# State-space mixer: the pair's rotation, additions and scan in place in PSUM on VectorE, the products for the transposed matrix on GpSimd

## The chip, the cores and the metric

One core of one Trainium2 chip runs one launch of the kernel. The metric is the device time of the launch in microseconds (us).

## The reference

One inference step of a model of two layers. Layer 0 mixes tokens by a state-space mixer (S5), layer 1 by a Fourier mixer; each mixer is followed by a gated feed-forward network with a convolution. There are 1152 tokens (128 of a context, 1024 of a sample) of 1024 channels. Only the S5 mixer is touched:

```python
def s5_direction(u, lam_re, lam_im, log_dt, b_re, b_im, c_re, c_im, h0, reverse):
    ...
    abar = jnp.exp(lam * dt)
    bbar = ((abar - 1.0) / lam)[..., None] * bmat
    bu = jnp.einsum('blgc,gpc->blgp', u.astype(jnp.complex64), bbar)
    ...
    _, h = lax.associative_scan(_linear_recurrence, (a, bu), axis=1, reverse=reverse)
    y = jnp.real(jnp.einsum('gcp,blgp->blgc', cmat, h))
```

So in each of 64 groups of 16 channels, a complex state h of 64 elements runs along the sequence as h = abar h + bu, once forwards and once backwards; y is the sum over both directions, and the last states are outputs too. After it come a gelu, the matmul `z = y @ w_glu` (GLU), and the rest of the network.

## The kernel before

**Tiling.** Tokens are taken in chunks of 8. The input of a group is then a tile u of 128 partitions (8 tokens x 16 channels) by 146 columns (`KW`: 144 chunks and two more for the ends). The eight groups of a block are worked off as four *pairs* of groups; 8 blocks of 4 pairs are 32 pairs, numbered i = 4b + pr. The two groups of a pair lie in the two halves of the 128 partitions (64 states each); each tile has both directions (dr) and the real and the imaginary part (r).

**What a block needs first** (`tables`, `make_ca`, `make_p`, `make_t`, `make_u`). The tables cs and sn (cosine and sine of the phase per chunk: VectorE computes and wraps the phase, L1306, L1307, L980, L981; ScalarE takes the absolute value wa, L1312, and the sines, L1320); Bbar (tiles Bb and Bx, L1381 to L1383 and what follows); CA (the output matrix times powers of abar, on GpSimd, L1365 to L1369); the products P of Bbar with powers of abar (VectorE, L1409 and six of 512 elements on L1414, three for each half of the block), which TensorE transposes (L1422) and ScalarE copies to PT (L1425); T, the part of y that stays within a chunk (64 small matmuls L1444, copies kc L1454 to L1456 on ScalarE, an addition on GpSimd, stored to DRAM and read back by SP's queue); and the next u (`make_u`, copies hb on ScalarE, L1476).

**A pair.** `vmm`: sixteen matmuls make V = PT u (L1499) in a two-bank PSUM tile; two such tiles take turns. `vin`: VectorE multiplies V by the sine and by the cosine (B L1521, A L1522), GpSimd adds the products into the SBUF tile Z (L1523, L1524), ScalarE makes the decay tile dec (L1514, needs no data of the pair), copies the final states out (Fin, L1526), GpSimd clears a column (L1527), ScalarE writes the initial states (L1528). The rotation thus takes the phase out, so that what is left is a real recurrence. `vout`: VectorE scans Z into S (L1538: one instruction over 592 elements, both parts and directions one behind the other, with zeros in dec and the Z columns at the borders) and rotates back, C1 and C2 (L1543 to L1545). `wmm`: TensorE makes y from C, CA, T and u (L1561), and ScalarE copies it to ysb (L1567).

**What sets the order.** The schedule is by hand: each engine runs its instructions in the order in which the program issues them, and waits at semaphores. `Ssm.run` is the loop. Step i issues the V matmuls of pairs up to i + 2 (as soon as their PT is there), `vin(i + 1)`, `wmm(i - 1)`, then what the next blocks need by pr (pr 0: tables, first half of the products, pr 1: second half, pr 2: Bbar, pr 3: the next u), then `vout(i)`, and behind it the work called late:

```python
late = tr[0] + tb[2:3]                            # pr 0: transposes of half 0, sines
late = tr[1] + tb[3:]                             # pr 1: transposes of half 1, cosines
late = [lambda: self.make_t(b + 1)()]             # pr 2: T of the next block
```

From pair 27 on, the loop also issues first work of the next stage (`early`), and when the last `wmm` is issued, the GLU follows (L199).

Of the kernel before, what the change touches and what calls it, by code (L numbers as in the profile page):

```python
# [959 lines left out]


class Ssm:
    def __init__(self, net, k_dram, y_dram, out_re, out_im):
# [147 lines left out]
    def start(self):  # L1111

        nc, sp = self.nc, self.sp

        mask = self.mask = sp.tile([128, 2, 148], F32, name="mask")
        nc.gpsimd.memset(mask, 1.0)
        for dr, p in ((0, 0), (0, 130), (1, 0), (1, 18)):
            nc.gpsimd.memset(mask[:, dr, p:p + 1], 0.0)
        self.Z = [sp.tile([128, 2, 2, 148], F32, name=f"Z{i}") for i in range(2)]
        for z in self.Z:  # L1120
            nc.gpsimd.memset(z[:, :, :, 147], 0.0)
            nc.gpsimd.memset(z[:, :, :, 0], 0.0)
        self.Fin = sp.tile([128, 2, NG], F32, name="Fin")
        self.hb = self.sg.tile([128, 8, KW], F32, name="hb")
        nc.gpsimd.memset(self.hb[:, :, 128:130], 0.0)
# [24 lines left out]
    def powers(self, gs, beside=None):  # L1150
# [3 lines left out]
        n = gs.stop - gs.start  # L1154
        PR = sp.tile([128, n, 9], F32, tag="A", bufs=2, name="PR")
        PI = sp.tile([128, n, 9], F32, tag="B", bufs=2, name="PI")
        t = sp.tile([128, n, 8], F32, tag="C1", bufs=2, name="q1")
        V.memset(PR[:, :, 0], 1.0)
# [85 lines left out]
    def ada_mm(self, n, p):  # L1244

        two = len(p.shape) == 3
        ps, q = ([p[:, g, 292:420] for g in range(2)], p[:, 0, 420:424]) if two else ([p[:, :128], p[:, 128:256]], p[:, 256:260])
        w = self.wa.pop(n)
        for v, o in enumerate(ps):
            for k in range(8):  # L1250
                j = 32 * (k % 4)
                self.nc.tensor.matmul(o[j:j + 32], lhsT=self.n.SC[:, k], rhs=w[:, k, 128 * v:128 * v + 128], start=k < 4,
                                      stop=k >= 4)
        m = self.sg.tile([128, 256], F32, tag="m", bufs=2, name="m_ada")
        if two:
            self.nc.scalar.activation(m.rearrange("p (v f) -> p v f", v=2), p[:, :, 292:420], AF.Copy)
        else:
            self.nc.scalar.activation(m, p[:, :256], AF.Copy)
        self.m_ada.append((n, q, m))
# [135 lines left out]
    def make_p(self, b):  # L1395
# [6 lines left out]
        x = [t[:, :, None, :].to_broadcast([128, 8, 8, 16]) for t in (Bb[:, 0, :, 0], Bx[:, 1], Bx[:, 0])]  # L1402
        qs, Ps = [], {}

        def prod(h, i):
            def f():
                if not qs:
                    qs.append(self.sg.tile([128, 8, 8], F32, tag="gs", bufs=1, name="gs"))
                    V.tensor_tensor(qs[0], self.G[:, 0, gs], self.G[:, 1, gs], OP.add)  # L1409
                if i == 0:  # L1410
                    Ps[h] = self.sg.tile([128, 3, 4, 8, 16], F32, tag="P", bufs=1, name="P")
                g = (qs[0], self.G[:, 1, gs], self.G[:, 0, gs])[i]
                hs = slice(4 * h, 4 * h + 4)
                V.tensor_tensor(Ps[h][:, i], g[:, hs, :, None].to_broadcast([128, 4, 8, 16]), x[i][:, hs], OP.mult)  # L1414
            return f
# [74 lines left out]
    def vmm(self, i):  # L1490
# [4 lines left out]
        for dr in range(2):  # L1495
            for ri in range(2):
                for a in range(2):
                    r, x = slice(64 * a, 64 * a + 64), u[:, 2 * pr + a]
                    nc.tensor.matmul(V[r, dr, ri * KW:(ri + 1) * KW], lhsT=PT[pr // 2][:, ri, 2 * (pr % 2) + dr, r],  # L1499
                                     rhs=x[:, ::-1] if dr else x, start=True, stop=True)  # L1500
        self.vd[i] = V
        if 1 < i < 7:
            self.ada_mm(i + 1, V)
            if i < 5:
                self.ada_load(i + 3)

    def vin(self, i):
        nc, sp = self.nc, self.sp
        b, pr = divmod(i, 4)
        cs, sn = self.tab[b]  # L1510
        V = self.vd.pop(i)
        dec = self.sp.tile([128, 2, 2, 148], F32, tag="dec", bufs=2, name="dec")
        for dr in range(2):
            nc.scalar.activation(dec[:, :, dr], self.mask[:, None, dr].to_broadcast([128, 2, 148]), AF.Copy,  # L1514
                                 scale=self.r8[:, 2 * i + dr:2 * i + dr + 1])
        A = sp.tile([128, 2, 2, KW], F32, tag="A", bufs=2, name="A")
        B = sp.tile([128, 2, 2, KW], F32, tag="B", bufs=2, name="B")
        Z = self.Z[i % 2]
        v = V[:, :, :2 * KW].rearrange("p g (r k) -> p g r k", r=2)
        bc = lambda t: t[:, 2 * pr:2 * pr + 2, 1:147][:, :, None, :].to_broadcast([128, 2, 2, KW])  # L1520
        nc.vector.tensor_tensor(B, v, bc(sn), OP.mult)  # L1521
        nc.vector.tensor_tensor(A, v, bc(cs), OP.mult)  # L1522
        nc.gpsimd.tensor_tensor(Z[:, 0, :, 1:147], A[:, :, 0], B[:, :, 1], OP.add)  # L1523
        nc.gpsimd.tensor_tensor(Z[:, 1, :, 1:147], A[:, :, 1], B[:, :, 0], OP.subtract)  # L1524
        zf = Z.rearrange("p r d k -> p r (d k)")
        nc.scalar.activation(self.Fin[:, :, 2 * i:2 * i + 2], zf[:, :, 129:166:36], AF.Copy)  # L1526
        nc.gpsimd.memset(Z[:, :, 0, 130], 0.0)  # L1527
        nc.scalar.activation(zf[:, :, 0:167:166], self.h0[:, :, 2 * i:2 * i + 2], AF.Copy)  # L1528
        self.zd[i] = (Z, dec)

    def vout(self, i):
        nc, sp = self.nc, self.sp
        b, pr = divmod(i, 4)
        cs, sn = self.tab[b]
        Z, dec = self.zd.pop(i)
        S = sp.tile([128, 2, 2, 148], F32, tag="S", bufs=2, name="S")
        f = lambda t: t.rearrange("p r d k -> p (r d k)")
        nc.vector.tensor_tensor_scan(f(S), f(dec), f(Z), 0.0, OP.mult, OP.add)  # L1538
        C1 = sp.tile([128, 2, 2, KW], F32, tag="C1", bufs=2, name="C1")
# [41 lines left out]
    def run(self):  # L1581
        self.TB = 2
        for nm in ("tab", "BC", "xb", "CA", "Bb", "Bx", "PT", "T", "U", "vd", "zd", "cd", "ysb"):
            setattr(self, nm, {})
# [51 lines left out]
        n = 32  # L1636
        nv, ready = 2, {0}
        for i in range(n + 1):
            b, pr = divmod(i, 4)
            n1, n2 = b + 1 < 8, b + 2 < 8  # L1640
            while nv < n and nv <= i + 2 and nv // 4 in ready:
                self.vmm(nv)
                nv += 1
            if i + 1 < n:
                self.vin(i + 1)
            if i:
                self.wmm(i - 1)
# [31 lines left out]
            if pr == 1:  # L1679
                if n1:  # L1680
                    call(pp[1])
                    late = tr[1] + tb[3:]
                    if not n2:
                        late.append(lambda: self.make_t(b + 1)())
                    ready.add(b + 1)
                if not b:
# [5 lines left out]
            if pr == 2:  # L1692
                if n1 and n2:
                    late = [lambda: self.make_t(b + 1)()]
                if n2:
# [6 lines left out]
            if pr == 3 and n2:  # L1702
                self.make_u(b + 2)
                pl = ca[4:] + [ends]
                if b + 3 < 8:
                    self.load_x(b + 3)
            call(pl[:1])
            self.vout(i)
            call(pl[1:])
            if i == n - 1:  # L1710
# [156 lines left out]
```

## Time and profile before

| | before |
|---|---|
| median of 3 runs | 2461.51 us (2460.70 to 2462.96) |
| the profiled execution | 2462.09 us |
| its span | 2460.3 us |
| its mean granted TensorE clock | 0.978 |
| TensorE matmuls, busy | 2315.1 us (94%) |
| VectorE, busy | 1562.1 us (63%) |
| ScalarE, busy | 857.3 us (35%) |
| GpSimd, busy | 754.2 us (31%) |

The span runs from the first to the last instruction that the profile shows; the execution's own time is 1.8 us longer. The shares are means over the whole launch: the mixer's 32 pairs lie between about 48 and 347 us, where VectorE is busiest, and behind them TensorE works nearly without a gap. A time in the trace counts from the start of the span. In the rows, PE is TensorE, DVE is VectorE, ACT ScalarE, POOL GpSimd; a tile's row reads output <- inputs, with partitions x elements.

### The profile page before, as it was taken

To read this page: it belongs to the slowest core of one execution; us is meant where nothing else is said; L and a number is where in the kernel's file an instruction comes from. 1 tells how busy PE (TensorE), PEld (TensorE's weight loads), DVE (VectorE), ACT (ScalarE), POOL (GpSimd) and SP (SyncE) were. 2 spreads that over 40 slices of the span, in tenths; PEclk is the share of its full clock that TensorE was granted. 3 is DMA by queue.
4 is the path that set the end of the run, shared out by engine and by line. 5 is a ranking of instruction groups with operands and counts; after the bars stand their busy time and mean duration, and the time that the engine had idled before them with its cause. 6 is when DMAs were issued, how large, how long until landed. Compare 5 with 4: busy or idle time off the path is not lost.

```text
span 2460.3 us, 35710 instructions
## 1 busy us (share of the span) xinstructions
PE 2315.1 (94%) x14754; PEld 2229.3 (91%) x14754; DVE 1562.1 (63%) x2385; ACT 857.3 (35%) x1251; POOL 754.2 (31%) x517
## 2 busy tenths in 40 slices
PE   4787899999999999999999999999999999999996
PEld 3676789778999999999999989899999999999996
DVE  8999977888555553555535574954554545545456
ACT  4444463234422233222322354442233222332234
POOL 6667631345211221112211253621122111221124
PEclk8888899999999999999999999999999999999998
DMA  6323278573101111011110121111111101111012
GB/s 213 122 59 81 75 206 296 198 246 110 51 27 43 43 52 44 26 43 43 52 44 27 61 97 36 52 46 34 42 52 45 42 27 43 52 43 41 29 44 77
DMA packets 94522, 182.33 MB, mean 74 GB/s; under 512 B 16948, under 2 KB 57204, under 8 KB 93336
## 3 DMA queue, kind: packets, MB, share of 16 engines
q1 hardware_dynamic: 90824, 170.67, 22.0%
q0 software_dynamic: 2096, 6.62, 0.8%
q8 instruction: 117, 1.92, 0.3%
q10 hardware_dynamic: 1440, 2.75, 0.3%
q14 instruction: 45, 0.37, 0.0%
HBM read 163.70 MB, written 11.53 MB: 71 GB/s over the span
## 4 chain that ended last, share of the span: by engine, by line
PE 69%; DVE 22%; issue 4%; ACT 1%; DMA 1%; POOL 1%; SPq 1%; DVEq 0%; ACTq 0%; POOLq 0%
PE acc L199 64%; DVE c L308 3%; DVE S L1538 2%; DVE P L1414 2%; PE f L839 2%; DVE dh L602 1%; DVE dl L602 1%; DVE X L916 1%; DVE C L1545 1%; DVE C L1543 1%; DVE h L222 1%; PE f L749 1%; DVE X L363 1%; DVE X L364 1%; DVE B L1521 1%
## 5 line engine op out<-in xcount | busy, mean ns | idle before, releaser
L199 PE MATMUL acc<-h,uh 128*128 128x384 f32 (+1 forms) x4992 | 1014.9, 338 | 0.5 <-ACT ysb L1567 0.5
L199 PEld LDWEIGHTS acc<-h,uh 128*128 128x128 f32 x4992 | 884.9, 188 | 15.3 <-issue 12.3
L183 POOL TENSOR_TENSOR ul<-raw,uh 128x1024 fp32r<-128x1024 f32 x104 | 280.1, 2693 | 1238.8 <-ACT uh L182 1238.8
L199 PE MATMUL acc<-h,ul 128*128 128x384 f32 (+1 forms) x2496 | 571.2, 337 | 0.0
L308 DVE SCALAR_TENSOR_TENSOR c<-t,cw,c 128x896 f32<-128x896 f32 x704 | 347.2, 562 | 202.6 <-ACT c L305 202.6
L199 PEld LDWEIGHTS acc<-h,ul 128*128 128x128 f32 x2496 | 448.2, 189 | 0.0
L182 ACT ACTIVATE uh<-raw 128x1024 fp32r<-128x1024 f32 x108 | 113.7, 1053 | 544.7 <-PE acc L199 505.5
L300 DVE COPY wb<-acc 128x2 f32<-128x2 f32 x88 | 13.9, 158 | 406.0 <-PE acc L199 406.0
L363 DVE SCALAR_TENSOR_TENSOR X<-acc,MOD,X 128x768 f32<-128x768 f32 x168 | 169.7, 1010 | 118.3 <-PE acc L199 118.3
L199 PE MATMUL acc<-gh,dh 128*128 128x384 f32 x960 | 220.7, 337 | 18.4 <-DVE X L365 18.4
L199 PE MATMUL acc<-gl,dh 128*128 128x384 f32 x960 | 218.5, 335 | 0.0
L199 PE MATMUL acc<-gh,dl 128*128 128x384 f32 x960 | 218.2, 334 | 0.0
L199 PEld LDWEIGHTS acc<-gh,dh 128*128 128x128 f32 x960 | 168.8, 188 | 26.9 <-PE acc L199 23.6
L199 PEld LDWEIGHTS acc<-gh,dl 128*128 128x128 f32 x960 | 171.4, 188 | 0.0
L199 PEld LDWEIGHTS acc<-gl,dh 128*128 128x128 f32 x960 | 171.2, 188 | 0.0
L336 ACT ACTIVATE gh<-c 128x1152 fp32r<-128x1152 f32 x44 | 51.4, 1169 | 329.2 <-DVE c L331 290.9
L303 ACT ACTIVATE t<-t,wb 128x1024 f32<-128x1024 f32 x88 | 101.4, 1152 | 152.6 <-DVE t L301 152.6
L183 POOL TENSOR_TENSOR dl<-raw,dh 128x1024 fp32r<-128x1024 f32 x40 | 99.8, 2514 | 165.3 <-ACT dh L182 165.3
L305 ACT ACTIVATE c<-t,cb,cw 128x1152 f32<-128x1152 f32 x88 | 118.8, 1351 | 2.9
L301 DVE TENSOR_TENSOR t<-acc,R 128x1152 f32<-128x1152 f32 x88 | 118.6, 1348 | 0.0
L326 ACT ACTIVATE c<-c 128x1152 f32<-128x1152 f32 x44 | 51.4, 1167 | 152.9 <-DVE c L308 152.9
L1561 PE MATMUL y<-C,CA 64*128 64x146 f32 x1024 | 77.6, 305 | 14.1 <-DVE C L1543 14.1
(324 smaller groups left out, 2765.4 us busy)
## 6 DMA issues: line engine op xcount, KB each, us to landing
raw<-w_up SPq DMA_DIRECT2D x88, 512.0 KB, 3.6
w_ada<-w_ada SPq DMA_DIRECT2D x80, 512.0 KB, 4.7
raw<-w_down SPq DMA_DIRECT2D x44, 512.0 KB, 3.6
w_ada<-w_ada SPq DMA_DIRECT2D x8, 1024.0 KB, 6.4
raw<-w_glu SPq DMA_DIRECT2D x16, 512.0 KB, 4.7
u<-hb SPq DMA_DIRECT2D x64, 73.0 KB, 2.8
y_scratch<-ysb SPq DMA_DIRECT2D x8, 584.0 KB, 3.4
xt<-x SPq DMA_DIRECT2D x9, 512.0 KB, 8.4
```

What stands on the lines that cost most here:

```text
L182: nc.scalar.activation(hi, raw, AF.Copy)
L183: (E or nc.gpsimd).tensor_tensor(lo, raw, hi.bitcast(F32), OP.subtract)
L199: mm(outs[j], lhsT=w, rhs=r[j], start=first and i == 0, stop=last and i == 2)
L301: nc.vector.tensor_tensor(t.rearrange("p (a b) -> p a b", a=3), p[:, :, :384], self.R.rearrange("p (a b) -> p a b", a=3), OP.mult)
L303: nc.scalar.activation(t[:, :NS], t[:, :NS], AF.Identity, bias=wb[:, 0:1])
L305: nc.scalar.activation(c, t, AF.Identity, bias=cb[:, ui:ui + 1], scale=w(1))
L308: nc.vector.scalar_tensor_tensor(o, a, w(i), o, op0=OP.mult, op1=OP.add)
L326: nc.scalar.activation(c, c, AF.Silu)
L336: nc.scalar.activation(gh, c, AF.Copy)
L363: nc.vector.scalar_tensor_tensor(v, p[:, 0:2, :384], s(0), v, op0=OP.mult, op1=OP.add)
L602: nc.vector.scalar_tensor_tensor(o, i, a, o, op0=OP.mult, op1=OP.add)
L1561: nc.tensor.matmul(yp[:, a, :KW], lhsT=CA[64 * a:64 * a + 64, ca, 2 * pr + dr, 1:9].rearrange("p a b -> p (a b)"), rhs=x[:, ::-1] if dr el ...
```

## The change

`view` takes 592 contiguous elements of the two-bank tile V, from element V0 = 216 on: the real part of both directions ends the first bank, the imaginary part begins the second, and every direction has 148 columns, two of them gaps. All steps of a pair work in that view:

- ScalarE zeroes the gaps (one instruction of 4 x 2 elements, L1527 of the changed kernel).
- `vin`: B = V times sine goes to SBUF (L1532), V times cosine back into V (L1533), and the two additions, now on VectorE, take V and B into V (L1534, L1535). ScalarE copies Fin out (L1537), clears the column (L1538) and writes the initial states (L1539).
- `scan`, now a function of its own, scans V in place (L1543); `vout` reads the states from V (L1554 to L1556).
- Z, A and S are gone, and B has one buffer. dec has two more zeros.

The order of a step becomes: V matmuls of pair i + 1 alone (if not issued yet), `scan(i)`, `vin(i + 1)`, `vout(i)`, `wmm(i - 1)`, then the next blocks' work. The products P are issued on GpSimd for blocks 2 to 7 (L1412, L1417) and stay on VectorE for blocks 0 and 1. The transposes of the second half move from pr 1 to pr 2, right ahead of `make_t`; T of block 7 moves from pair 25 to pair 26. The small columns of the modulation matmuls (`ada_mm`), which share the tile V in the first pairs, move to the free places of its banks, with two copies for one. The tiles of the powers (`powers`) get places of their own.

```diff
 def ada_mm(self, n, p):
-        ps, q = ([p[:, g, 292:420] for g in range(2)], p[:, 0, 420:424]) if two else ...
+        ps, q = ([p[:, 0, 0:128], p[:, 1, 300:428]], p[:, 0, 128:132]) if two else ...
...
-            self.nc.scalar.activation(m.rearrange("p (v f) -> p v f", v=2), p[:, :, 292:420], AF.Copy)
+            for v in range(2):
+                self.nc.scalar.activation(m[:, 128 * v:128 * v + 128], ps[v], AF.Copy)
 def make_p(self, b):
+        E = nc.gpsimd if b > 1 else V
...
-                    V.tensor_tensor(qs[0], self.G[:, 0, gs], self.G[:, 1, gs], OP.add)
+                    E.tensor_tensor(qs[0], self.G[:, 0, gs], self.G[:, 1, gs], OP.add)
...
-                V.tensor_tensor(Ps[h][:, i], g[:, hs, :, None].to_broadcast([128, 4, 8, 16]), x[i][:, hs], OP.mult)
+                E.tensor_tensor(Ps[h][:, i], g[:, hs, :, None].to_broadcast([128, 4, 8, 16]), x[i][:, hs], OP.mult)
 def vmm(self, i):
+                    o = 148 * dr + 1 + (0 if ri else V0)
+                    nc.tensor.matmul(V[r, ri, o:o + KW], lhsT=PT[pr // 2][:, ri, 2 * (pr % 2) + dr, r],
+    def view(self, V):
+        return V.rearrange("p g k -> p (g k)")[:, V0:V0 + 592]
 def vin(self, i):
+        f = V.rearrange("p g k -> p (g k)")
+        nc.scalar.activation(f[:, V0 + 147:V0 + 147 + 592].rearrange("p (s k) -> p s k", k=148)[:, :, 0:2],
+                             self.zero[:, None, :].to_broadcast([128, 4, 2]), AF.Copy)
...
         nc.vector.tensor_tensor(B, v, bc(sn), OP.mult)
-        nc.vector.tensor_tensor(A, v, bc(cs), OP.mult)
-        nc.gpsimd.tensor_tensor(Z[:, 0, :, 1:147], A[:, :, 0], B[:, :, 1], OP.add)
-        nc.gpsimd.tensor_tensor(Z[:, 1, :, 1:147], A[:, :, 1], B[:, :, 0], OP.subtract)
+        nc.vector.tensor_tensor(v, v, bc(cs), OP.mult)
+        nc.vector.tensor_tensor(v[:, 0], v[:, 0], B[:, 1], OP.add)
+        nc.vector.tensor_tensor(v[:, 1], v[:, 1], B[:, 0], OP.subtract)
...
-        nc.gpsimd.memset(Z[:, :, 0, 130], 0.0)
+        nc.scalar.activation(zf[:, :, 130], self.zero, AF.Copy)
+    def scan(self, i):
+        S = self.view(self.vd[i])
+        self.nc.vector.tensor_tensor_scan(S, self.dec.pop(i).rearrange("p r d k -> p (r d k)"), S, 0.0, OP.mult, OP.add)
 def run(self):
-            while nv < n and nv <= i + 2 and nv // 4 in ready:
+            if nv < n and nv <= i + 1:
                 self.vmm(nv)
                 nv += 1
+            if i < n:
+                self.scan(i)
             if i + 1 < n:
                 self.vin(i + 1)
+            if i < n:
+                self.vout(i)
             if i:
                 self.wmm(i - 1)
...
             if pr == 1:
-                    late = tr[1] + tb[3:]
-                    if not n2:
-                        late.append(lambda: self.make_t(b + 1)())
-                    ready.add(b + 1)
+                    late = tb[3:]
...
             if pr == 2:
-                if n1 and n2:
-                    late = [lambda: self.make_t(b + 1)()]
+                if n1:
+                    late = tr[1] + [lambda: self.make_t(b + 1)()]
```

In the rows of order, a number behind a tile's name is its buffer, the bracket names the engines or DMA queues at whose semaphores the instruction waits, and the scan stands as SCALAR_TENSOR_TENSOR.

**Order, first place: VectorE around a block's tables.** Before, from the rotation of the block's second pair to the first product behind the scan of its first:

```order
L1521 TENSOR_TENSOR B<-V,sn 128x584 [waits PE_49]
L1522 TENSOR_TENSOR A<-V,cs 128x584
L1306 COPY w<-W_173 128x8x18
L1307 TENSOR_TENSOR w<-W_173,ph_174 128x8x112
L980 TENSOR_SCALAR wa<-w 128x8x112 [waits DVE_49]
L981 TENSOR_TENSOR w<-w,wa 128x8x112 [waits DVE_49]
L1409 TENSOR_TENSOR gs<-Gt 128x64
L1414 TENSOR_TENSOR P<-gs,Bb 128x512 [waits DVE_49]
L1414 TENSOR_TENSOR P<-Gt,Bx 128x512 x2
L1538 SCALAR_TENSOR_TENSOR S<-dec,Z_133 128x592 [waits Activation_49,Pool_49]
L1543 TENSOR_TENSOR C_2419<-S,cs 128x584 [waits DVE_49,PE_49]
```

Now, from the last addition of the second pair to the third pair's rotation (the tables' rows, L1308 to L984, are those of L1306 to L981 above):

```order
L1535 TENSOR_TENSOR V<-V,B 128x2x146 [waits DVE_49]
L1554 TENSOR_TENSOR C_1967<-V,cs 128x584
L1555 TENSOR_TENSOR C_1968<-V,sn 128x292
L1556 SCALAR_TENSOR_TENSOR C_1968<-V,sn 128x292
L1308 COPY w<-W_171 128x8x18
L1309 TENSOR_TENSOR w<-W_171,ph_172 128x8x112
L983 TENSOR_SCALAR wa<-w 128x8x112 [waits DVE_49]
L984 TENSOR_TENSOR w<-w,wa 128x8x112 [waits DVE_49]
L1543 SCALAR_TENSOR_TENSOR V<-dec,V 128x592 [waits Activation_49]
L1532 TENSOR_TENSOR B<-V,sn 128x584 [waits Activation_49]
L1533 TENSOR_TENSOR V<-V,cs 128x4x146
```

The scan of a pair now stands ahead of the next pair's rotation; the products are gone from VectorE, two additions have come in, and the rotation (L1532), which waited for TensorE, waits for ScalarE's zeroing of V.

**Order, second place: ScalarE in the same stretch.** Before, from the second pair's initial states to the third's dec and what stands behind it:

```order
L1528 ACTIVATE Z_134<-sm 128x2x2
L1567 ACTIVATE ysb<-y 128x292 [waits PE_49]
L1312 ACTIVATE wa<-w 128x1040 [waits DVE_49]
L1425 ACTIVATE PT<-misc 128x512 [waits PE_49] x2
L1320 ACTIVATE sn<-w 128x4x129
L1320 ACTIVATE sn<-w 128x4x18
L1320 ACTIVATE sn<-w 128x4x129
L1320 ACTIVATE sn<-w 128x4x18
L1514 ACTIVATE dec<-mask,r_306 128x2x148 [waits DVE_49]
L1514 ACTIVATE dec<-mask,r_306 128x2x148
L1526 ACTIVATE Fin<-Z_133 128x2x2 [waits Pool_49]
```

Now, from the second pair's initial states to the zeroing of the third pair's V and Fin:

```order
L1539 ACTIVATE V<-sm 128x2x2 [waits Activation_49]
L1578 ACTIVATE ysb<-y 128x292 [waits PE_49]
L1314 ACTIVATE wa<-w 128x1040 [waits DVE_49]
L1428 ACTIVATE PT<-misc 128x512 [waits PE_49] x2
L1322 ACTIVATE sn<-w 128x4x129
L1322 ACTIVATE sn<-w 128x4x18
L1322 ACTIVATE sn<-w 128x4x129
L1322 ACTIVATE sn<-w 128x4x18
L1524 ACTIVATE dec<-mask,r_304 128x2x148 x2
L1527 ACTIVATE V<-zero 128x4x2 [waits PE_49]
L1537 ACTIVATE Fin<-V 128x2x2 [waits DVE_49,Activation_49]
```

The row L1527 stands behind wa, both PT copies, the four sines and the two dec; nothing of VectorE waited for this part of the queue before, except the scan for dec, Fin and the initial states.

**Order, third place: ScalarE around T, from the block's third pair to its fourth.** Before (the second half's two PT copies stood a pair ahead of this):

```order
L1567 ACTIVATE ysb<-y 128x292 [waits PE_49]
L1392 ACTIVATE Bb<-Bb 128x16x16 [waits DVE_49]
L1454 ACTIVATE kc<-misc 128x128 [waits DMAHW3_49,PE_49]
L1455 ACTIVATE k_1839<-misc 128x16
L1456 ACTIVATE kc<-misc 128x112
L1454 ACTIVATE kc<-misc 128x128 [waits PE_49]
L1455 ACTIVATE k_1839<-misc 128x16
L1456 ACTIVATE kc<-misc 128x112
L1514 ACTIVATE dec<-mask,r_306 128x2x148 [waits DVE_49]
L1514 ACTIVATE dec<-mask,r_306 128x2x148
```

Now:

```order
L1578 ACTIVATE ysb<-y 128x292 [waits PE_49]
L1394 ACTIVATE Bb<-Bb 128x16x16 [waits DVE_49,Pool_49]
L1428 ACTIVATE PT<-misc 128x512 [waits PE_49] x2
L1457 ACTIVATE kc<-misc 128x128 [waits DMAHW3_49,PE_49]
L1458 ACTIVATE k_1822<-misc 128x16
L1459 ACTIVATE kc<-misc 128x112
L1457 ACTIVATE kc<-misc 128x128 [waits PE_49]
L1458 ACTIVATE k_1822<-misc 128x16
L1459 ACTIVATE kc<-misc 128x112
L1524 ACTIVATE dec<-mask,r_304 128x2x148 x2
L1527 ACTIVATE V<-zero 128x4x2 [waits PE_49]
```

The PT copies of the second half now stand between Bbar's copy and kc, and all of it is ahead of the zeroing (L1527) on which VectorE's next rotation waits.

## Rows read from the trace of the kernel before

**Rows 1.** Timeline of VectorE's scans and TensorE: start, us, engine, line, operation, tiles

```profile
114.25 1.58 DVE L1538 TENSOR_TENSOR_SCAN S<-dec,Z 128x592 f32<-128x592 f32 x1
...
269.04 1.58 DVE L1538 TENSOR_TENSOR_SCAN S<-dec,Z 128x592 f32<-128x592 f32 x1
...
305.44 1.39 DVE L1538 TENSOR_TENSOR_SCAN S<-dec,Z 128x592 f32<-128x592 f32 x1
...
312.53 1.38 DVE L1538 TENSOR_TENSOR_SCAN S<-dec,Z 128x592 f32<-128x592 f32 x1
...
316.72 1.38 DVE L1538 TENSOR_TENSOR_SCAN S<-dec,Z 128x592 f32<-128x592 f32 x1
...
326.69 1.37 DVE L1538 TENSOR_TENSOR_SCAN S<-dec,Z 128x592 f32<-128x592 f32 x1
...
347.40 1.33 PE L199 MATMUL acc<-h,uh 128*128 128x384 f32 x6 [0.51 <-ACT ysb L1567]
```

**Rows 2.** Timeline of VectorE: tables of block 7, then Bbar and the scan behind

```profile
245.80 0.27 DVE L1381 TENSOR_TENSOR Bb<-Bm,beta 128x128 f32<-128x128 f32 x1
...
247.82 3.11 DVE L1538 TENSOR_TENSOR_SCAN S<-dec,Z 128x592 f32<-128x592 f32 x1
...
299.69 0.22 DVE L1306 COPY w<-W 128x144 f32<-128x144 f32 x1
...
303.39 0.21 DVE L1409 TENSOR_TENSOR gs<-Gt 128x64 f32<-128x64 f32 x1
```

**Rows 3.** VectorE's lines apart: duration in ns, least/median/most, first and last start

```profile
L1521 DVE TENSOR_TENSOR B<-V,sn x32: 750/753/768, 48.3 to 335.4; 128x584 f32<-128x584 f32 x32
...
L1543 DVE TENSOR_TENSOR C<-S,cs x32: 767/928/2748, 60.7 to 342.0; 128x584 f32<-128x584 f32 x32
...
L1545 DVE SCALAR_TENSOR_TENSOR C<-S,sn x32: 448/454/2629, 65.4 to 343.2; 128x292 f32<-128x292 f32 x32
...
L364 DVE SCALAR_TENSOR_TENSOR X<-acc,MOD,X x168: 462/473/478, 676.9 to 2410.1; 128x256 f32<-128x256 f32 x168
```

**Rows 4.** Timeline of GpSimd beside that scan

```profile
247.67 2.02 POOL L1367 TENSOR_TENSOR CA<-Qt,Cx 128x1024 f32<-128x1024 f32 x1
```

**Rows 5.** Timeline of ScalarE, blocks 3 to 5

```profile
218.73 0.45 ACT L1476 ACTIVATE hb<-misc,b,a 128x128 f32<-128x128 f32 x1
...
221.69 0.96 ACT L1514 ACTIVATE dec<-mask,r 128x296 f32<-128x296 f32 x2
...
226.13 1.07 ACT L1312 ACTIVATE wa<-w 128x1040 f32<-128x1040 f32 x1 [0.35 <-DVE w L981]
...
232.28 0.60 ACT L1425 ACTIVATE PT<-misc 128x512 f32<-128x512 f32 x1 [1.74 <-PE misc L1422]
...
232.77 1.46 ACT L1320 ACTIVATE sn<-w 128x516 f32<-128x516 f32 x4
...
239.82 1.83 ACT L1320 ACTIVATE cs<-wa,hpi 128x516 f32<-128x516 f32 x4
...
248.09 0.40 ACT L1392 ACTIVATE Bb<-Bb 128x256 f32<-128x256 f32 x1
...
251.52 0.28 ACT L1454 ACTIVATE kc<-misc 128x128 f32<-128x128 f32 x1 [3.03 <-PE misc L1444]
...
252.36 0.98 ACT L1514 ACTIVATE dec<-mask,r 128x296 f32<-128x296 f32 x2
```

**Rows 6.** Timeline of TensorE, blocks 4 and 5

```profile
232.17 2.22 PE L1499 MATMUL V<-u,PT 128*64 128x146 f32 x16
...
237.33 1.97 PE L1422 MATMUL misc<-ident,P 128*128 128x128 f32 x16
...
247.10 4.84 PE L1444 MATMUL misc<-CA,Bb 64*32 64x128 f32 x64
...
251.88 1.22 PE L1499 MATMUL V<-u,PT 128*64 128x146 f32 x16
...
253.72 2.26 PE L1561 MATMUL y<-C,CA 64*128 64x146 f32 x32
```

## What the change will do to the time

> **What bounds the kernel now.** Everything the change touches lies in the mixer, which ends when the matmuls of the next stage start at 347.4 us [rows 1]. From there on TensorE sets the time, so a change of the mixer's end is a change of the total. The scans on VectorE's timeline are its milestones, one for each of 32 pairs, four to a block. From pair 4's scan to pair 20's, 114.25 to 269.04 us, four blocks take 154.8 us, 38.7 us each; block 5 takes 36.4, block 6 21.25 us, and from pair 28's scan (326.69) to the end of the mixer it is 20.7 us [rows 1].
>
> VectorE has no idle stretch in a block, but much of its time is not work. A pair without contention takes 4.19 us from scan to scan (312.53 to 316.72) [rows 1]. The tables of a block take 3.7 us (299.69 to 303.39), one half of its products with their sum 2.05 us (303.39 to 305.44), the other half 1.8 by the same durations, Bbar 2.0 us (245.80 to 247.82) [rows 2]. Together 4 x 4.19 + 3.7 + 2.05 + 1.8 + 2.0 = 26.3 us. The other 12.4 us of the 38.7 are VectorE instructions that stand still. The first product after the scan (L1543, two operands in SBUF) takes between 767 and 2748 ns, the last one (L1545) between 448 and 2629, while the rotation, of the same 584 elements but with V from PSUM, takes 750 to 768 in all 32 pairs [rows 3]. One case shows who holds it up: GpSimd's product for CA runs from 247.67 to 249.69 us [rows 4], and the scan begun at 247.82 takes 3.11 instead of 1.38 us: it ends 1.24 us after GpSimd [rows 2]. In block 6 GpSimd prepares no CA, and the block is short. So the bound is VectorE plus its contention with GpSimd.
>
> **The change, term by term.** (1) *Work on VectorE.* A pair gains two additions of 292 elements at 0.37 us (start to start, as L1545 does when undisturbed), two waits on its own results at 0.1, and loses nothing: 4.19 + 0.94, say 5.2 us. The six products leave for blocks 2 to 7. A block's work becomes 4 x 5.2 + 3.7 + 2.0 = 26.5 us, as before.
>
> (2) *Contention.* All eight instructions of a pair now have one operand in PSUM, as the rotation has, whose 32 runs differ by 18 ns. I take the 12.4 us as gone, but for what is inside the 3.7 and 2.0.
>
> (3) *PSUM as source and target.* No VectorE instruction of the trace writes PSUM. Reading it costs between 14 ns less than SBUF (least 753 against 767 for 584 elements; 753 is the median) and some 50 ns more (L364: 462 for 256 elements from PSUM; L1545: 448 for 292 from SBUF, so 37 ns more by size) [rows 3]. I take the nearest, the same form and size: nothing. At 50 ns for seven uses in 32 pairs it would be +11 us. [...]
>
> (4) *The new wait.* Before, the rotation of pair i+1 waited for TensorE alone, and ScalarE was free to lag. Now it waits for ScalarE's zeroing of V (order, above), which stands in ScalarE's queue behind everything the pair before left there. Behind the rotation stand the additions, the products of pair i and the next scan, and V's two buffers hold TensorE to one pair ahead. Four of these waits recur per block:
>
> - *After the tables* (pair 4b+1): from VectorE's last table instruction, wa 1.0, two PT copies 1.0, four sines 1.4, dec 0.9, zero 0.2 = 4.5 us by start-to-start times [rows 5]. VectorE has the scan meanwhile, 1.5. Idle 3.0.
> - *Pair 4b+2*: from the pair's last addition, Fin, zero and h0 0.5 (four elements each, taken below kc's 0.28), ysb 0.4 (292 elements, below PT's 0.6), four cosines 1.8, dec 0.9, zero 0.2 = 3.8 [rows 5]; VectorE has the two C's and the scan, 3.0. Idle 0.8.
> - *Pair 4b+3*: the transposes of the second half and T's matmuls are now both issued after this block's Bbar. From Bbar's sum: ScalarE's copy 0.4, first PT copy 0.6, T's 64 matmuls 4.3 (4.84 in the row; 64 passes at V's 1.22/16 us, for 128 columns instead of 146, make 4.3), kc 0.9, dec 0.9, zero 0.2, hand-overs 0.4 = 7.7 [rows 5, 6]. VectorE has 0.7 of Bx and the scan, 2.2. Idle 5.5.
> - *Pair 4b+4*: make_u's copies and CA's ends, 218.73 to 221.69, 3.0 us, dec 0.9, zero 0.2, ysb 0.3, behind y's 2.9 us on TensorE (253.1 to 255.98) = 7.3 from the end of V's matmuls [rows 5, 6]; VectorE has 5.4. Idle 1.9.
>
> Together 11.2 us: a block of 26.5 + 11.2 = 37.7 us. The contention is exchanged for waits.
>
> (5) *The sum.* Blocks 1 to 4: 4 x (37.7 - 38.7) = -4. Block 5: +1.3. Block 6 had neither contention nor Bbar: 24.5 work, then 3.0 + 0.8 + 1.9, and for pair 27 a TensorE chain of V 1.2, y 2.9, transposes 1.9, T 4.3, and on ScalarE 2.3 more, 12.6 against 7.5 on VectorE, 5.1: 35.3 - 0.6 (its tables run undisturbed) = 34.7 against 21.25, +13.4. Pairs 28 to 31: V's matmuls now start after the pair before the last is read, so a pair takes 1.5 + 0.2 + 3.7 = 5.4; three of them and some 5.5 to the end are 21.7 against 20.7, +1. Start and block 0, which I can't add up closely: the first rotation waits behind T's matmuls and copies, as pair 4b+3 does, so +5.5; block 0 trades contention for waits as blocks 1 to 4 do, but has the most two-SBUF work to free. I set them against each other: zero, give or take 6. [...] Sum: -4 + 1.3 + 13.4 + 1 + 0 + 4 = **+15.7 us** on the profiled execution's 2462.1 us (0.6 above the median of the runs): **2478 us**.
>
> (6) *What costs nothing.* GpSimd loses 64 additions and 32 memsets and gets 36 products of 512 elements, each about half of the 2.02 us of a 1024-element product [rows 4], some 6 us a block: it fits, and each half is due a pair or more later. Its first half now stands behind the addition to k, which waits for kc; if it came late, the transposes would move by the same amount, 3 to 5 us. SP's queue keeps its order; T(7) is stored a pair later but used two pairs later, under the end of block 6. ScalarE's three small extra instructions of 0.2 us a pair are in the waits above.
>
> **The rivals.** *A: the waits stay short* (faster). If ScalarE reaches the zeroing before VectorE asks for it, a block is its 26.5 us of work: 4 x -12.2 - 9.9 + 2.6 + 1 is -55, about 2407 us; with half of the waits about 2443. For it: the rotation's times say that the contention does go. Against it: a queue in order cannot overtake, and the tables, PT and kc are ahead of the zeroing. It decides at waits of 8 us a block: below that the kernel gains. Chance 0.13.
> *B: an even trade.* Waits of 8 to 9 us instead of 11 in all six blocks: 2457 to 2467. For it: my chains have hand-overs of 0.1 us that nothing here measures. Chance 0.11.
> *C: dearer still.* PSUM at 50 ns or more a use (+11), contention of the tables and Bbar with a GpSimd that now runs products beside them (up to 2 us in six blocks, +12; the scan's row shows one of 1.7), T at 4.84 throughout (+3): 2500 to 2520. Against it: the flat rotation. Chance 0.10.
>
> **The numbers.** My forecast, waits that take the contention's place and a long block 6, has 0.66, and spans 2460 to 2505 by its own unknowns: block 0 give or take 6, the waits by 2 us a block less or more, PSUM up to +11. The range **2456 to 2506** adds most of B and leaves A and the far end of C out. About 0.2% is what a measurement of this kernel tells from no change. Faster by more is A, 0.13; within it is B, 0.11; slower is the forecast and C, 0.76.
>
> **What would show it.** Right: L1543 to L1545's successors (L1554 to L1556) flat at 0.75 and 0.45 us; VectorE idle before L1532 with ScalarE's L1527 as releaser, some 60 us in all; blocks 1 to 5 near 38 us and block 6 near 35. Wrong: no idle before L1532 (A), in which case block 6 stays near 24 us; or pair instructions that still vary by GpSimd's, or take over 0.85 us for 584 elements (C). If block 6 is long but blocks 1 to 5 come to 32 us, the sizes of the waits were wrong and the total is about the same.

## The result, and the profile after

The changed kernel takes 2499.60 us (median of 4 runs, 2498.64 to 2502.86) for 2462.12 before (4 runs): ratio 1.0155, 95% interval 1.0138 to 1.0173. It is slower, as forecast, and inside the range of 2456 to 2506, but by 37.5 us where the sum said 15.7. The mixer's end shows all of it: the GLU's first matmul starts at 384.69 us for 347.40 [rows 1]; the span is 2497.9 us for 2460.3.

| stretch (from scan to scan) | before | forecast | after |
|---|---|---|---|
| start and block 0, to pair 4's scan | 114.25 | +0 | 116.33 (+2.1) |
| blocks 1 to 5, to pair 24's | 191.2 | +0.8 | 206.4 (+15.2) |
| block 6, to pair 28's | 21.25 | +14.1 | 38.5 (+17.3) |
| pairs 28 to 31, to the GLU | 20.7 | +1 | 23.4 (+2.7) |
| behind the mixer (rest of the span) | 2112.9 | +0 | 2113.2 (+0.3) |

The sum's last term, +4 (rounded), is the author's estimate for a lower clock of TensorE, 0.7 us in each of six blocks, and stands in the rows of those blocks: before, V's sixteen matmuls at 232.17 and at 251.88 [rows 6] ran at granted clocks of 0.50 and 1.00. The scans do not cut the two kernels at the same place: before, the tables and the first half of the products of step 4b stand ahead of pair 4b's scan (for pair 24 from 299.69 to 305.44 us [rows 1] [rows 2]); now the tables stand behind it. So block 6's row holds no tables before and one set of them after, and the start's row the other way round; the sum of the rows is not touched.

VectorE's timeline of the changed kernel, with one whole block (block 4, pairs 16 to 19; start, us, line, tiles, in brackets the idle time before it and what ended it):

```profile
116.33 1.40 DVE L1543 TENSOR_TENSOR_SCAN V<-dec,V 128x592 f32<-128x592 f32 x1 [0.58 <-ACT a L1273]
...
240.87 1.39 DVE L1543 TENSOR_TENSOR_SCAN V<-dec,V 128x592 f32<-128x592 f32 x1
244.49 0.77 DVE L1532 TENSOR_TENSOR B<-V,sn 128x584 f32<-128x584 f32 x1 [2.23 <-ACT V L1527]
...
248.26 1.02 DVE L1308 COPY w<-W 128x144 f32<-128x144 f32 x1
249.20 1.95 DVE L1309 TENSOR_TENSOR w<-W,ph 128x896 f32<-128x896 f32 x1
251.19 1.36 DVE L983 TENSOR_SCALAR wa<-w 128x896 f32<-128x896 f32 x1
252.58 2.69 DVE L984 TENSOR_TENSOR w<-w,wa 128x896 f32<-128x896 f32 x1
255.20 1.38 DVE L1543 TENSOR_TENSOR_SCAN V<-dec,V 128x592 f32<-128x592 f32 x1
259.66 0.77 DVE L1532 TENSOR_TENSOR B<-V,sn 128x584 f32<-128x584 f32 x1 [3.08 <-ACT V L1527]
...
266.05 0.77 DVE L1532 TENSOR_TENSOR B<-V,sn 128x584 f32<-128x584 f32 x1 [1.23 <-ACT V L1527]
...
278.02 0.77 DVE L1532 TENSOR_TENSOR B<-V,sn 128x584 f32<-128x584 f32 x1 [5.47 <-ACT V L1527]
...
281.79 1.39 DVE L1543 TENSOR_TENSOR_SCAN V<-dec,V 128x592 f32<-128x592 f32 x1
...
322.74 1.39 DVE L1543 TENSOR_TENSOR_SCAN V<-dec,V 128x592 f32<-128x592 f32 x1
...
361.28 1.39 DVE L1543 TENSOR_TENSOR_SCAN V<-dec,V 128x592 f32<-128x592 f32 x1
```

Two things are to be seen. The block's four waits, 2.23 + 3.08 + 1.23 + 5.47 = 12.0 us, stand where the prediction put them, with ScalarE's zeroing as releaser; over the mixer they are 101.6 us in 31 waits. And the four table instructions, from 248.26 to 255.20, take 6.9 us, where they took 3.7 before [rows 2]. The other 22 of the block's 40.9 us are four pairs of 5.16 us and Bbar's 1.3.

What stands ahead of the zeroing is on ScalarE's timeline (the wait of 3.08 us), and for the long wait on TensorE's, whose V (L1503) is issued behind T (L1447):

```profile
255.31 1.07 ACT L1314 ACTIVATE wa<-w 128x1040 f32<-128x1040 f32 x1 [7.35 <-DVE w L984]
256.29 1.07 ACT L1428 ACTIVATE PT<-misc 128x512 f32<-128x512 f32 x2
257.24 1.47 ACT L1322 ACTIVATE sn<-w 128x516 f32<-128x516 f32 x4
258.60 0.96 ACT L1524 ACTIVATE dec<-mask,r 128x296 f32<-128x296 f32 x2
259.46 0.17 ACT L1527 ACTIVATE V<-zero 128x8 f32<-128x8 f32 x1
```

```profile
263.58 2.21 PE L1503 MATMUL V<-u,PT 128*64 128x146 f32 x16 [11.07 <-DVE C L1556]
...
271.90 4.61 PE L1447 MATMUL misc<-CA,Bb 64*32 64x128 f32 x64
276.44 1.22 PE L1503 MATMUL V<-u,PT 128*64 128x146 f32 x16
...
384.69 1.33 PE L199 MATMUL acc<-h,uh 128*128 128x384 f32 x6 [0.51 <-ACT ysb L1578]
```

Wa, PT, sines and dec take from 255.31 to 259.46, as long as the zeroing is late. V's matmuls end at 277.66 (276.44 + 1.22), and VectorE goes on at 278.02: there ScalarE only ends the wait that TensorE makes.

VectorE's lines of the changed kernel one by one (least/median/most in ns), with those of the tables behind:

```profile
L1532 DVE TENSOR_TENSOR B<-V,sn x32: 766/767/769, 58.7 to 374.2; 128x584 f32<-128x584 f32 x32
L1534 DVE TENSOR_TENSOR V<-V,B x32: 470/471/471, 60.2 to 375.7; 128x292 f32<-128x292 f32 x32
L1543 DVE TENSOR_TENSOR_SCAN V<-dec,V x32: 1382/1386/1396, 65.3 to 378.0; 128x592 f32<-128x592 f32 x32
L1554 DVE TENSOR_TENSOR C<-V,cs x32: 755/756/767, 73.1 to 379.5; 128x584 f32<-128x584 f32 x32
...
L984 DVE TENSOR_TENSOR w<-w,wa x8: 1092/1894/3110, 37.4 to 334.5; 128x896 f32<-128x896 f32 x8
...
L983 DVE TENSOR_SCALAR wa<-w x8: 628/1361/2232, 36.5 to 333.1; 128x896 f32<-128x896 f32 x8
```

Every instruction with V in PSUM now takes the same time in all 32 pairs, to within 14 ns, where the first product behind the scan had taken between 767 and 2748 ns [rows 3]. The tables, whose tiles all lie in SBUF, vary by a factor of about three (L984: 1092 to 3110 ns). What runs beside them is on GpSimd's timeline of the same stretch:

```profile
248.14 1.05 POOL L1417 TENSOR_TENSOR P<-gs,Bb 128x512 f32<-128x512 f32 x1 [1.37 <-PE misc L1425]
249.15 2.91 POOL L1417 TENSOR_TENSOR P<-Gt,Bx 128x512 f32<-128x512 f32 x2
252.03 2.30 POOL L1367 TENSOR_TENSOR CA<-Qt,Cx 128x1024 f32<-128x1024 f32 x1
```

The second half's products wait for the transposes of the first half (their tile P has one buffer) and so start at 248.14, when VectorE starts its tables; CA follows. Before, GpSimd waited there for VectorE's product A and then ran the additions into Z beside the tables, on its timeline:

```profile
222.47 1.63 POOL L1523 TENSOR_TENSOR Z<-A,B 128x292 f32<-128x292 f32 x1 [1.75 <-DVE A L1522]
```

In block 1 of the changed kernel GpSimd's products start only at 128.71 us, behind the tables, and the same four instructions take 2.9 us on VectorE's timeline:

```profile
125.26 0.23 DVE L1308 COPY w<-W 128x144 f32<-128x144 f32 x1
...
128.20 1.39 DVE L1543 TENSOR_TENSOR_SCAN V<-dec,V 128x592 f32<-128x592 f32 x1
```

### The profile page after: what moved, and what is told of

Its sections match the earlier page's. It is cut to its first block, busy times and chain, and to the rows that moved or that the text cites. A ratio compares the mean times of both kernels' runs of the same rounds, so it can differ in the third digit from the quotient of the medians.

```text
span 2497.9 us, 35759 instructions
## 1 busy us (share of the span) xinstructions
PE 2311.4 (93%) x14754; PEld 2228.0 (89%) x14754; DVE 1499.9 (60%) x2407; ACT 868.4 (35%) x1320; POOL 697.0 (28%) x462
## 4 chain that ended last, share of the span: by engine, by line
PE 72%; DVE 17%; issue 4%; ACT 3%; DMA 1%; POOL 1%; DVEq 0%; ACTq 0%; POOLq 0%
PE acc L199 62%; DVE c L308 3%; DVE dl L602 2%; DVE dh L602 2%; PE f L839 2%; PE misc L1447 2%; DVE X L916 1%; PE y L1572 1%; DMA w_ada<-w_ada 1%; DVE h L222 1%; PE V L1503 1%; PE f L749 1%; DVE X L363 1%; DVE X L364 1%; PE misc L1425 1%
## 5 line engine op out<-in xcount | busy, mean ns | idle before, releaser
L1503 PE MATMUL V<-u,PT 128*64 128x146 f32 x512 | 45.7, 328 | 62.0 <-DVE C L1556 61.9
```

The source lines that it names most:

```text
L1503: nc.tensor.matmul(V[r, ri, o:o + KW], lhsT=PT[pr // 2][:, ri, 2 * (pr % 2) + dr, r], rhs=x[:, ::-1] if dr else x, start=True, stop=True)
```

## The experiments

The theories are W (the waits and the tables beside GpSimd), Q (ScalarE's queue is all of it), P (something else: instructions on PSUM, or the order), G (the products on GpSimd) and S (in the kernel before, GpSimd's additions contend).

**GpSimd's work left out: the tables.**

```diff
 def prod(h, i) / make_ca(b), for b > 3
-   E.tensor_tensor(...)        # products P, CA
+   (the tiles P and CA of block 3 are used again)
```

> The changed kernel, but GpSimd's products P and its CA of blocks 4 to 7 are left out (those of block 3 are used again), so that from block 3 on GpSimd has next to nothing to do while the tables run. Theory W: the tables' four instructions fall from 6.94 to 2.9 us, the four waits stay as they are, blocks 3 to 5 take 36.9 us for 40.9 and block 6 36.1 for 38.5: 2478 to 2488 us. Rival P (the tables are slow for another reason, as the order of the queue or the clock): they stay at 6.9 us, 2495 to 2503 us.

Measured: 2485.95 us (one run). VectorE's timeline of this run in its block 4, one block long from scan to scan:

```profile
233.54 1.38 DVE L1550 TENSOR_TENSOR_SCAN V<-dec,V 128x592 f32<-128x592 f32 x1
...
240.93 0.22 DVE L1308 COPY w<-W 128x144 f32<-128x144 f32 x1
241.07 1.09 DVE L1309 TENSOR_TENSOR w<-W,ph 128x896 f32<-128x896 f32 x1
242.19 0.63 DVE L983 TENSOR_SCALAR wa<-w 128x896 f32<-128x896 f32 x1
242.85 1.09 DVE L984 TENSOR_TENSOR w<-w,wa 128x896 f32<-128x896 f32 x1
243.86 1.39 DVE L1550 TENSOR_TENSOR_SCAN V<-dec,V 128x592 f32<-128x592 f32 x1
...
267.14 0.77 DVE L1539 TENSOR_TENSOR B<-V,sn 128x584 f32<-128x584 f32 x1 [5.92 <-ACT V L1534]
...
270.91 1.39 DVE L1550 TENSOR_TENSOR_SCAN V<-dec,V 128x592 f32<-128x592 f32 x1
```

The tables take 2.9 us, the block 37.4 for 40.9 us: 4.0 us come from the tables, 0.5 goes back into the longest wait (5.92 for 5.47). Block 6 is 37.5 us where W said 36.1, since its longest wait grows from 5.96 to 7.38. W holds, and P falls as far as the tables go.

**The products back on VectorE.**

```diff
-        E = nc.gpsimd if b > 1 else V
+        E = V
```

> The changed kernel with the products P of blocks 2 to 7 back on VectorE. Theory W (time went to waits for ScalarE and TensorE, 12.0 us a block, and to tables that run beside whatever GpSimd does, 6.9 us for 2.9): GpSimd's CA steps move up to where the products were and still stand beside the tables, so the tables stay at 4.5 us or more; the products (3.9 us a block) are partly covered by the waits, but the sines then stand behind a later PT. Within 8 us of the changed kernel, 2492 to 2508 us. Rival G (it is the products on GpSimd that made it slow): tables at 3 us, some 4 us a block back, 2475 to 2485 us.

Measured: 2518.52 us, ratio 1.0223 (1.0208 to 1.0238) to the kernel before: slower still, outside both expectations. In its timeline of VectorE the tables are about as long as in the changed kernel, 6.7 us for 6.9, since now CA stands beside them, as W said; but the products (1.8 and 2.1 us) are not covered. The waits of a block stay 11.8 us for 12.0, because the one after the tables grows from 3.08 to 4.56: ScalarE's PT copies come ahead of the sines and now wait for products that VectorE makes after the tables, and for transposes that take 3.97 us for 1.97, at a granted clock of 0.50 behind a gap of 9.9 us. A block is 44.2 us.

```profile
258.47 3.23 DVE L1309 TENSOR_TENSOR w<-W,ph 128x896 f32<-128x896 f32 x1
261.74 2.23 DVE L983 TENSOR_SCALAR wa<-w 128x896 f32<-128x896 f32 x1
...
273.02 0.77 DVE L1532 TENSOR_TENSOR B<-V,sn 128x584 f32<-128x584 f32 x1 [4.56 <-ACT V L1527]
```

G falls: in this order the products are better placed on GpSimd. And the tables meet GpSimd whether it runs the products or CA.

**The gaps zeroed once.** After a scan the gaps are still zero, so two V tiles that live through the mixer need the zeroing only in pairs 0 and 1.

```diff
-        V = self.pp.tile([128, 2, 512], F32, tag="V", bufs=2, name="V")
+        V = self.V2[i % 2]
...
+        if i < 2:
             nc.scalar.activation(f[:, V0 + 147:V0 + 147 + 592]...
```

> The changed kernel with two V tiles that live through the mixer and whose gaps are zeroed for the first two pairs only (the scan leaves them zero), so that VectorE's rotation waits for TensorE's V matmuls alone. Theory W: of the four waits of a block, the one after the tables (3.1 us) goes, the one at the next u (2.2) falls to 1.0 since V's matmuls end 1.2 us ahead of the zeroing there, and the other two (1.2 and 5.5) lose only 0.2 to 0.3 us each, because V's matmuls end just ahead of the zeroing (behind T on TensorE): some 4.8 us a block, and 5 at the start: 2462 to 2472 us. Rival Q (ScalarE's queue is all of it): the four waits vanish, 12 us a block, 2405 to 2425 us.

Measured: 2458.96 us (ratio to before 0.9981, 0.9972 to 0.9991), 3 us below W's range, and far from Q's. VectorE's timeline in block 4 shows which waits ScalarE's queue had made and which it had only ended:

```profile
219.81 1.39 DVE L1544 TENSOR_TENSOR_SCAN V<-dec,V 128x592 f32<-128x592 f32 x1
222.27 0.77 DVE L1533 TENSOR_TENSOR B<-V,sn 128x584 f32<-128x584 f32 x1 [1.07 <-PE V L1503]
...
237.90 0.77 DVE L1533 TENSOR_TENSOR B<-V,sn 128x584 f32<-128x584 f32 x1 [1.01 <-PE V L1503]
...
250.09 0.77 DVE L1533 TENSOR_TENSOR B<-V,sn 128x584 f32<-128x584 f32 x1 [5.71 <-PE V L1503]
...
253.87 1.39 DVE L1544 TENSOR_TENSOR_SCAN V<-dec,V 128x592 f32<-128x592 f32 x1
```

The wait after the tables is gone, the one at the next u is halved, and the two others stand, released by TensorE: 7.8 us for 12.0. The long one is T, issued ahead of V. The one of 1.01 us ends with V's matmuls, which take 2.21 us there for 1.22 (235.64 to 237.85, granted clock 0.50, behind a gap of 4.6 us): by these numbers it is about what TensorE's lower granted clock costs. The block is 34.1 us; the 2.6 us beyond the waits are tables of 4.4 instead of 6.9, since they meet GpSimd at another moment.

**The order alone, and both.** V's matmuls of pair i + 2, its dec and its zeroing go into step i:

```diff
-            if nv < n and nv <= i + 1:
-                self.vmm(nv)
...
             if i:
                 self.wmm(i - 1)
...
+            if i + 2 < n:
+                self.vmm(i + 2)
+                self.vprep(i + 2)
```

> The changed kernel in another order: V's matmuls of pair i + 2, its dec and its zeroing are issued in step i, behind the C products of pair i and ahead of the work for the next blocks (PT, sines, T, make_u). Theory W: three of the four waits shrink to about 0.3 us; the one at T moves a pair on, since T (with the transposes 6.6 us) and y's matmuls (3.0) stand ahead of the next V on TensorE, and is some 4.5 us: 5.4 us of waits a block for 12.0, 2445 to 2465 us. Rival P (VectorE's instructions on PSUM, not the waits, are what costs): no more than 5 us change, 2494 to 2504 us.

> Both: gaps zeroed once, and V's matmuls of pair i + 2 issued early. Theory W: as in the run with the order alone, with 0.2 to 0.3 us less in each wait: 2438 to 2462 us, VectorE's idle before the rotation some 4.5 us a block, all of it released by TensorE. Rival Q: nothing left to wait for, a block is its 28.9 us of work, 2405 to 2420 us.

Measured: 2439.80 us for the order alone (ratio 0.9903, 0.9888 to 0.9918) and 2434.98 us for both (0.9883, 0.9868 to 0.9897), 5 and 3 us below W's ranges; the second is 15 us above Q's. Both are faster than the kernel before, with the same instructions on PSUM as the changed kernel: as far as it holds instructions on PSUM dear, P is ruled out. W's wait behind T and y is there, but shorter (1.6 us for 4.5), because a new one ahead of it takes its place; VectorE's timeline of the run with both:

```profile
234.43 1.40 DVE L1547 TENSOR_TENSOR_SCAN V<-dec,V 128x592 f32<-128x592 f32 x1 [2.39 <-ACT V L1543]
237.44 0.77 DVE L1536 TENSOR_TENSOR B<-V,sn 128x584 f32<-128x584 f32 x1 [1.62 <-PE V L1503]
...
264.93 1.40 DVE L1547 TENSOR_TENSOR_SCAN V<-dec,V 128x592 f32<-128x592 f32 x1 [2.40 <-ACT V L1543]
```

The scan now waits for the initial states (L1543 there), which stand behind kc in ScalarE's queue; W had not named this wait. The block shown is 30.5 us.

**V ahead of y.** In the run with both, V's matmuls of pair i + 2 are put ahead of y's of pair i - 1, with three buffers for C1 and C2.

> As the run with both (gaps zeroed once, V's matmuls early), with V's matmuls of pair i + 2 ahead of y's of pair i - 1 on TensorE, and a third buffer for C1 and C2. Theory W: in the run with both, VectorE's wait of 1.6 us a block for the V behind T and y goes; the scan's wait of 2.4 us for the initial states behind kc in ScalarE's queue stays: 1.6 us a block less, 2420 to 2432 us. Rival: TensorE, with 28 us of work in a block of 30.5, now is late with y instead, and nothing is gained: 2432 to 2440 us.

Measured: 2449.60 us (0.9950, 0.9933 to 0.9966), 15 us worse than without. The wait behind T and y is gone, but VectorE's timeline shows the other one grown:

```profile
246.29 1.40 DVE L1547 TENSOR_TENSOR_SCAN V<-dec,V 128x592 f32<-128x592 f32 x1 [3.53 <-ACT V L1543]
```

A block is 31.0 us for 30.5, and 11 us are lost by pair 8 (its scan starts at 150.94 for 140.19), where the modulation's small steps (L1273), which TensorE and ScalarE hand to each other, hold up the rotation. That nothing is gained the rival had said; the loss is larger than its range (2432 to 2440), and most of it lies in the first blocks, which it did not name.

**Parts of the change in the kernel before.** First the products alone on GpSimd:

```diff
+        V = nc.gpsimd if b > 1 else V     # in make_p
```

> The kernel before with one part of the change: the products P of blocks 2 to 7 on GpSimd. Theory W: VectorE loses 3.9 us of products a block, and the 2 us for which they stood still, but GpSimd's queue gets 6 us more ahead of the additions into Z for which the scan waits, and the rest of the contention stays: a block of 34 to 40 us, 2435 to 2470 us, block 6 within 3 us of before. Rival G (products on GpSimd are what costs): 2475 us or more.

Measured: 2454.71 us (0.9974, 0.9965 to 0.9984), inside W's range, and G falls here too. But block 6 is 26.6 us for 21.25, where W allowed 3 us more, with a wait of 3.91 us for V behind T. And from 139.63 us on the tables take 5.1 to 6.0 us for 3.7: here, too, they run beside long products of GpSimd (CA's of 2.36 us at 286.49, for one). Then Z's additions alone on VectorE:

```diff
-        nc.gpsimd.tensor_tensor(Z[:, 0, :, 1:147], A[:, :, 0], B[:, :, 1], OP.add)
+        nc.vector.tensor_tensor(Z[:, 0, :, 1:147], A[:, :, 0], B[:, :, 1], OP.add)
```

> The kernel before with another part: the additions into Z on VectorE, but in SBUF and in the old order, with no zeroing and V's matmuls two pairs ahead. Theory W: contention hits instructions whose operands all lie in SBUF, and eight such of 0.37 us or more come to a block, while GpSimd loses some 8 us: 2 to 6 us a block more, block 6 some 3 us more, no waits before the rotation: 2470 to 2500 us. Rival S (what contends are the additions of GpSimd, and leaving them out frees VectorE without PSUM): 2400 to 2450 us.

Measured: 2464.74 us (1.0012, 1.0003 to 1.0022), short of W's range and far from S's. The additions cost nearly what GpSimd's smaller load gives back (a block is 38.9 us for 38.7). In both runs contention stays (in the second, more than half of these instructions run undisturbed), as the first product behind the scan shows, by the view of single lines (first the run with the products, then the one with the additions):

```profile
L1544 DVE TENSOR_TENSOR C<-S,cs x32: 766/1014/2735, 59.6 to 334.2; 128x584 f32<-128x584 f32 x32
```

```profile
L1543 DVE TENSOR_TENSOR C<-S,cs x32: 767/768/2678, 65.8 to 344.6; 128x584 f32<-128x584 f32 x32
```

So neither part by itself makes the loss, and neither ends the contention of the pairs. That leaves the third part, the pair in PSUM, which was not run by itself; the flat rows of the changed kernel show that with it the contention of the pairs is gone.

**Two more steps from the run with both.** The copies kc go behind the next pair's initial states; then also the transposes of the second half back to pr 1.

```diff
-                    late = tr[1] + [lambda: self.make_t(b + 1)()]
+                    late = tr[1] + [lambda: kept.append(self.make_t(b + 1))]
...
                 self.vin(i + 1)
+            if kept:
+                kept.pop()()
```

> As the run with both (gaps zeroed once, V's matmuls early), with the copies kc of T put behind the next pair's initial states in ScalarE's queue. Theory W: the scan's wait of 2.4 us a block for the initial states behind kc goes, the wait of 1.6 us for V behind T and y stays: 2418 to 2428 us. Rival: T then comes later, and TensorE waits for it ahead of y, so that nothing or less than a third is gained: 2431 us or more.

Measured: 2436.09 us (0.9895, 0.9878 to 0.9911): no gain, so W's range missed and the rival's number came. Its mechanism did not, since TensorE goes from T to y without a gap (233.61). The scan waits no more, but the wait for V behind T and y is longer by about as much, on VectorE's timeline:

```profile
237.76 0.77 DVE L1536 TENSOR_TENSOR B<-V,sn 128x584 f32<-128x584 f32 x1 [4.55 <-PE V L1503]
```

The two had stood in one another's shadow: what ends last is TensorE's T (4.6 us), y and V.

> The same, and the transposes of the second half back from pr 2 to pr 1, so that T starts 2 us earlier on TensorE. Theory W: the wait for V behind T falls by 0.9 us a block at most, 2411 to 2426 us. Rival: the cosines then stand behind the transposes and their products on GpSimd, which come 3 us later than VectorE's did, and the gain is lost: 2426 us or more.

Measured: 2422.18 us (0.9837, 0.9823 to 0.9852), inside W's range and the fastest version of the study, 40.6 us ahead of the kernel before. The wait behind T fell by 1.5 us in blocks 5 and 6 where W allowed 0.9 at most. VectorE's timeline of that version:

```profile
247.06 1.40 DVE L1547 TENSOR_TENSOR_SCAN V<-dec,V 128x592 f32<-128x592 f32 x1 [0.96 <-ACT V L1543]
...
256.60 0.77 DVE L1536 TENSOR_TENSOR B<-V,sn 128x584 f32<-128x584 f32 x1 [3.09 <-PE V L1503]
```

What is left in blocks 5 and 6 is one wait of 3 us behind T and y, and one of 1 us behind the cosines.

## Why the prediction was half right

- **What bounds the mixer, and where the waits come from:** right. The four waits are 2.2, 3.1, 1.2 and 5.5 us; the steps said 1.9, 3.0, 0.8 and 5.5. The runs also bear out the reason, an in-order queue: with the same instructions in another order the kernel is some 60 us faster (of block 4's 8.2 us, 6.2 are waits and 1.9 are tables that meet GpSimd at another moment).
- **Step 1 and step 3, VectorE's work and the price of PSUM:** right. A pair takes 5.16 us for the 5.2 said, the rotation 767 ns for 753, the product from S 756 for 767. The 0.1 us for each of two waits on its own results, for which the prediction named no row, is 0.12 (L1533 to L1534 start to start 0.80 us for 0.68, L1534 to L1535 0.50 for 0.38).
- **Step 2, the contention:** this step failed. It took the 12.4 us "as gone, but for what is inside the 3.7 and 2.0", and so held the tables at 3.7 us. They have no tile in PSUM, and in the new order long products of GpSimd ran beside them: 6.9 us in blocks 3 to 5, 8.2 in block 2, 5.4 in block 6, and 2.9 in block 1, where GpSimd stood idle. Against the sum's 3.7 (3.1 in block 6) that is 15.7 us, of the 21.8 by which the change exceeds the sum. The 3.7 came from rows in which only short additions of GpSimd ran beside the tables (1.62 and 1.08 us, from 299.85 on). The price was in the text, but as part of rival C, at "up to 2 us in six blocks" and a chance of 0.10. The run without GpSimd's work shows that it is this. L984, whose tiles all lie in SBUF, takes 1.09 us alone and 2.69 beside GpSimd's products (252.58), while the pairs, with V in PSUM, stay within 14 ns; and GpSimd is held up in turn, its two products on L1417 taking 2.91 us beside the tables for 2.07 beside a pair (at 240.32). By what mechanism the two hold each other up, no run here shows.
- **Step 4, other waits:** too small by some 8 us over blocks 1 to 5, half of it in block 1 (15.5 us for 11.2), where ScalarE also does the modulation's copies, which the step had left out, and T takes 5.88 us for 4.61 behind a gap of TensorE of 2.8 us (145.73, granted clock 0.71). In the sum most of the 8 is made up by the 3.5 us for TensorE's lower clock in these blocks and by a Bbar of 1.3 us for 2.0. The sign of "some 60 us in all" was below the steps' own 67 in blocks 1 to 6; those came to 76, and 24 more lie at the start and in block 0.
- **Step 5:** block 6's long wait was 5.96 us for 5.1; the start lost 6.4 us and block 0 gained 4.4, so they nearly cancel, as assumed (+2.1). One reading was wrong: block 6's 21.25 us are short not only for want of CA, but because the tables and products that stand ahead of its first scan (5.75 us) fall into the stretch before. The forecast counted a set of tables into the new block 6 and took none off the start by name; the start's "zero, give or take 6" covered it, which is luck as much as reckoning. The 0.7 us a block in the sum's +4 is a size that no run shows. What the traces show is a lower granted clock, over blocks 1 to 5 0.85 for 0.89 before: behind a gap of 11 us V and y take 6.5 us (263.58 to 270.07, granted clock 0.50 up to 265.80 and 0.66 behind that) for 4.1 at a granted clock of 1.00 (242.06 to 246.16), and the transposes and T follow y without a gap. T starts at 271.90 and, waiting for Bbar's copy on ScalarE, could not have started before 271.15; so an estimate from these rows is 0.75 us of the long wait at most, which the sum's 0.7 a block is near.
- **Rivals:** A was ruled out by VectorE's idle time before L1532. The point from which it decides, 8 us of waits a block, would have been right only with tables of 3.7 us. B fell, since the waits were 12 us a block and not 8 to 9. C's time all but came (2499.6 for 2500 to 2520), but of its three terms only the contention: PSUM cost nothing (a pair 5.16 us for 5.2), and T took 4.61 us. That the time still lies in the range owes to the room left for PSUM and block 0, not to a right price of the tables.

## What to carry to other kernels

Before an instruction of the busiest engine is made to wait for a short one of another engine, read what stands ahead of the short one in its queue: the same in-place pair loses 37 us in one order, gains 23 in another, and gains 41 with the zeroing gone and T's steps spread. When GpSimd's work grows or moves, look not only at whether it fits, but at which VectorE instructions with all tiles in SBUF will run beside it: here those with an operand in PSUM stayed flat, to within 14 ns, and the tables were held up, by the products or by CA (6.9 and 6.7 us for 2.9). Of two waits that end near each other, removing the later one gives only their difference: with kc moved the scan's 2.40 us went, and the wait for V rose from 1.62 to 4.55.

## What the runs showed that was not expected

Two of the tables' instructions that read a single tensor, from SBUF to SBUF, are held up too: the copy (L1308) takes 0.22 us alone and 1.02 beside a product of GpSimd, the one with a scalar (L983) 0.63 and 1.36 to 2.23. The rotation (L1532), which also reads the sine from SBUF and writes B there but takes V from PSUM, is not: it takes 766 to 769 ns in 32 pairs, and at 244.49 0.77 us beside GpSimd's L1366 (1.93 us, from 243.59). With V in PSUM as an operand, on whichever side, no line of the pair varies by more than 14 ns in 32 pairs of the changed kernel. And the products on GpSimd, alone in the kernel before, made it faster by 0.26%, though its pairs went on standing still beside them.
